# Modulation by pairs of tiles, split of the first weights, context's decays as columns, and a later place for the second modulation's first part

## The chip, the cores and the metric

The kernel runs on one core of a Trainium2 chip. The metric is the device time of one execution in microseconds; a comparison uses the median over several executions. TensorE (PE) multiplies, VectorE (DVE), ScalarE (ACT) and GpSimd (POOL) do elementwise work, and SyncE (SP) issues most of the transfers. Each engine works through its own row of instructions in order.

## The reference

One layer of a hybrid backbone with width D = 1024, 1024 latent tokens and 256 context tokens, 1280 in all. Cut to what matters:

```python
mod_x = silu(c) @ w_ada + b_ada            # six parts: sh1, sc1, g1, sh2, sc2, g2
mod_c = silu(c_ctx) @ w_ada + b_ada
px = modulate(rms_norm(x, norm1_w), sh1, sc1) @ w_in      # modulate: h * (1 + scale) + shift
pc = modulate(rms_norm(ctx, norm1_w), csh1, csc1) @ w_in
dn_c, s_f, s_b = gated_deltanet(pc[..., :DN_IN], ..., zero, zero)   # q, k, v, z, decays a, b
dn_x, _, _     = gated_deltanet(px[..., :DN_IN], ..., s_f, s_b)     # both directions, chunks of 64
na_x = neighborhood_attention(...)          # q, k with RMS norm, window keys and all context keys
x = x + g1 * (concat([dn_x, na_x]) @ w_out)
x = x + g2 * swiglu(modulate(rms_norm(x, norm2_w), sh2, sc2), w_ffn_in, w_ffn_out)
```

## The kernel before

Tokens lie along the free axis: x is eight tiles `xt0` to `xt7` of 128 features by 1280 tokens. A product in full precision is made of three in fp32r: each weight is split into `whi` (a cast, on ACT) and `wlo` (the rest, on POOL), each operand into `hh` and `hl`, and a block sums hh·whi, hl·whi and hh·wlo over the eight tiles (`mm_part`, L395).

*First stage.* SP loads c2, prm and the x tiles, then the first modulation's weights `wada` (eight tiles of 1 MB) and the raw weights `fraw` of the first two blocks; ACT's queue loads cw, qkw, onw, adt, cst and the masks. ACT squares each tile (L670), DVE adds the squares (L672), TensorE sums them over the partitions with ones (L675), ACT takes Ln and Exp of that. `ada(q)` makes a quarter of the first modulation: 16 products into one bank (L651), a copy `arow` on ACT (L654), a turn by four small products with `sel` (L657), an addition of the bias on DVE (L659). With the weights as they lie, ada(0) and ada(2) give scales, ada(1) and ada(3) shifts, each for four tiles. Then tile by tile: xt (L689) and hl (L692) on DVE, hh (L690) on ACT, and the products of the blocks `first` = k0, k1. SP's transfers take turns on a fixed set of semaphores, so an issue can wait for an earlier transfer of another queue.

*Jobs.* From then on a list of jobs is worked through: k2, k3, `Wide z 1`, (here `inv` = 5) nk0 to nk2, z0, nk3, nq0 to nq2, q0 to q3, nv0, v0, nv1, v1 to v3, nq3. A `Block` makes 128 features by all tokens. A `Wide` makes tokens by 256 or 264 columns (L578), with the tokens as stationary operand. The last 16 columns of z's second half are the decays `ab`; for the first two tiles of tokens, which are context, z itself is not needed, and the product is narrow (16 columns, L594). Beside the jobs run `Background` generators: `bg` (inverses of the blocks, decay tables, and from then on the preparations of the scans: `pr` products, kk L902, y L921), and `bg2`, the first four quarters of the second modulation. A quarter (`modulation`) loads eight tiles `wad` of 128 x 512, multiplies them by silu(c) and adds them up on DVE (L230, L232), and ends with four small products (L217) and an addition of the bias (modp, L219):

```python
        bg2.add(modulation(pools(bg2s, "adp", "left"), range(4), bank))
...
            if n == inv:
                bg2.drain()
```

The rest of the second modulation (quarters 4 to 7) follows in the last stages. Then come the scans and the attention (about 640 to 875 us), the output products with the gated output `oacc` (L1052, L1170; its pool `sp1`), and the feed-forward products, to the end. The scheduler that sets each engine's row may place an instruction earlier or later than it is written, as far as its operands allow.

Of the kernel before, what the change touches and what calls it, by code (L numbers as in the profile page):

```python
# [9 lines left out]
F32 = mybir.dt.float32  # L10
# [77 lines left out]
def hybrid(ctx, tc, a, dbg):  # L88
# [30 lines left out]
    sp.dma_start(c2, a["c2"])  # L119
    sp.dma_start(prm, a["prm"])  # L120
# [6 lines left out]
    act.dma_start(cw, a["cw"])  # L127
    qkw = const("qkw", [128, 2])
    act.dma_start(qkw, a["qkw"])
    onw = const("onw", [128, 1])  # L130
    act.dma_start(onw, a["onw"])
    adt = const("adt", [128, 16])
    act.dma_start(adt, a["adt"].rearrange("o d -> (o d)").partition_broadcast(128))
# [68 lines left out]
    def modulation(adp, qs, bank):  # L202
# [18 lines left out]
        for _ in range(3):  # L221
            fetch()
        prev = None
        for q in qs:
            acc2 = adp.tile([128, 512], F32, name="acc2", tag="acc2", bufs=2)
# [11 lines left out]
        for _ in range(6):  # L237
            yield
        reduce(qs[-1], prev)
# [127 lines left out]
    with ExitStack() as bs:  # L367
# [30 lines left out]
        class Block:  # L398
# [7 lines left out]
            def prefetch(self, raw=None):  # L406
# [3 lines left out]
                self.w = load_w(src, raw=raw)  # L410
# [143 lines left out]
        class Wide:  # L554
# [27 lines left out]
            def tiles(self):  # L582
# [26 lines left out]
        with ExitStack() as xs:  # L609
            xp = pools(xs, "xp", "left")  # L610
            xt = []
            act.dma_start(cst, a["cst"])
            masks = xp.tile([128, 4, 128], F32, name="masks", tag="masks")
            act.dma_start(masks, a["masks"])
# [12 lines left out]
            for j in range(4):  # L627
                load_ada(j)
            raws = [xp.tile([128, KT, 128], F32, name=f"fraw{i}", tag=f"fraw{i}") for i in range(2)]
            for i in range(2):  # L630
                sp.dma_start(raws[i], a["w_conv"][4 + i])
            for j in range(4, 8):
                load_ada(j)
            sel = xp.tile([128, 2], F32, name="sel", tag="sel")
            dve.tensor_reduce(sel, ident.rearrange("p (c i) -> p i c", i=32)[:, 0:2], AX.X, OP.add)
# [3 lines left out]
            act.copy(mr[:, 4], ident)  # L639
            for d in range(2):  # L640
                act.mul(mneg[:, d], masks[:, d], -1.0e30)
            act.copy(mr[:, 0:4], masks)
            rs = xp.tile([128, T], F32, name="rs", tag="rs")
            acc = xp.tile([128, T], F32, name="acc", tag="acc")
            def ada(q):
# [10 lines left out]
                for b in range(4):  # L656
                    pe.matmul(p[:, 2 * b:2 * b + 2], row[:, b * 128:(b + 1) * 128], sel, start=True, stop=True)  # L657
                b0 = 4 * (q // 2) + 8 * (1 - q % 2)
                dve.tensor_tensor(mod1[:, b0:b0 + 4], p[:, 0:8].rearrange("p (b c) -> p b c", c=2),  # L659
                                  bada[:, b0:b0 + 4].rearrange("p (b c) -> p b c", c=1).to_broadcast([128, 4, 2]),  # L660
                                  OP.add)
                if q % 2 == 0:
                    b = b0 - 8
                    dve.scalar_tensor_tensor(w1s[:, b:b + 4], mod1[:, b0:b0 + 4], 1.0,
                                             n1w[:, b:b + 4].rearrange("p (b c) -> p b c", c=1).to_broadcast(
                                                 [128, 4, 2]), op0=OP.add, op1=OP.mult)

            for k in range(KT):
                sq = xp.tile([128, T], F32, name="sq", tag="sq", bufs=2)
                act.activation(sq if k else acc, xt[k], AF.Square)  # L670
                if k:
                    dve.tensor_tensor(acc, acc, sq, OP.add)  # L672
            for s0, n in SEGS:
                p = bank()
                pe.matmul(p[:, :n], M[C_ONE], acc[:, s0:s0 + n], start=True, stop=True)  # L675
                act.activation(rs[:, s0:s0 + n], p[:, :n], AF.Ln, bias=b_eps, scale=1.0 / D)
            act.activation(rs, rs, AF.Exp, scale=-0.5)
            first[0].prefetch(raws[0])
            ada(0)
            ada(1)  # L680
            first[1].prefetch(raws[1])
            for k in range(KT):
# [13 lines left out]
                if k == 1:  # L696
# [976 lines left out]
```

## Time and profile before

| | before |
|---|---|
| runs | 1618.23, 1617.94, 1624.84 us, median 1618.23 |
| profiled execution | 1618.78 us, its span 1617.0 us |
| mean granted clock of TensorE | 0.979 |
| TensorE busy | 1512.7 us |
| DVE, ACT, POOL busy | 1039.2, 706.2, 210.8 us |
| first dense products of k0 (chain) | 45.66 us |

The page gives busy times, and 40 slices of the span, 40.4 us each. The chain follows the work that ended last back to its releasers; a row there holds start, duration and what ran. A row of the timeline holds start, duration, engine, line, operation and tiles, and in brackets the idle time before it and what ended it. A row of grouped lines ends with total, mean in ns, and idle time before. A row of windows holds the stretch, its length, the busy time of PE, the weight loads, DVE, ACT and POOL with their counts, then the granted clock, the share of DMA and GB/s.

### The profile page before, as it was taken

To read this page: it belongs to the slowest core of one execution; us is meant where nothing else is said; L and a number is where in the kernel's file an instruction comes from. 1 tells how busy PE (TensorE), PEld (TensorE's weight loads), DVE (VectorE), ACT (ScalarE), POOL (GpSimd) and SP (SyncE) were. 2 spreads that over 40 slices of the span, in tenths; PEclk is the share of its full clock that TensorE was granted. 3 is DMA by queue.
4 is the path that set the end of the run, shared out by engine and by line. 5 is a ranking of instruction groups with operands and counts; after the bars stand their busy time and mean duration, and the time that the engine had idled before them with its cause. 6 is when DMAs were issued, how large, how long until landed. Compare 5 with 4: busy or idle time off the path is not lost.

```text
span 1617.0 us, 24090 instructions
## 1 busy us (share of the span) xinstructions
PE 1512.7 (94%) x8642; PEld 1275.1 (79%) x8642; DVE 1039.2 (64%) x1931; ACT 706.2 (44%) x1341; POOL 210.8 (13%) x279
## 2 busy tenths in 40 slices
PE   2899899999989798999898999999999999999999
PEld 1689787778888786888787787888888888888887
DVE  4785678445264467577898638966656656679652
ACT  5353363663332234666674337433333333444441
POOL 0144611422232320111110000000000000000000
PEclk9898999999999899999999999999999999999999
DMA  9267121545346528999853910532223333698742
GB/s 370 89 209 218 56 76 40 177 129 173 120 126 194 185 95 212 312 282 283 234 178 119 324 46 33 196 105 98 98 98 110 101 109 113 231 365 307 253 157 85
DMA packets 206407, 271.03 MB, mean 168 GB/s; under 512 B 15952, under 2 KB 115792, under 8 KB 205264
## 3 DMA queue, kind: packets, MB, share of 16 engines
q1 hardware_dynamic: 200240, 264.14, 50.2%
q10 hardware_dynamic: 6048, 5.35, 1.0%
q8 instruction: 68, 1.11, 0.3%
q14 instruction: 51, 0.42, 0.1%
HBM read 204.68 MB, written 68.94 MB: 169 GB/s over the span
## 4 chain that ended last, share of the span: by engine, by line
PE 76%; DVE 10%; ACT 5%; DMA 4%; issue 2%; POOL 1%; SPq 0%; ACTq 0%; DVEq 0%; POOLq 0%
PE ps L1249 26%; PE ps L1592 13%; PE blk L395 11%; PE blk L578 4%; PE pr L920 3%; PE ps L1376 3%; PE sc L316 2%; PE sc L306 2%; PE sc L294 2%; DVE N L826 1%; DMA at<-qk_d 1%; DMA wad<-wa 1%; DVE tt L824 1%; DVE cacc L451 1%; PE pr L911 1%
## 5 line engine op out<-in xcount | busy, mean ns | idle before, releaser
L395 PE MATMUL blk<-hh,whi 128*128 128x512 f32 (+1 forms) x416 | 123.9, 390 | 1.4 <-ACT hh L690 1.0
L1310 ACT CAST uhi<-wq 128x512 fp32r<-128x512 f32 x101 | 60.4, 621 | 140.7 <-issue 61.6
L395 PE MATMUL blk<-hl,whi 128*128 128x512 f32 (+1 forms) x416 | 117.1, 374 | 5.0 <-DVE hl L692 5.0
L1310 ACT CAST uhi<-ws 128x512 fp32r<-128x512 f32 x91 | 54.7, 622 | 152.9 <-PE ps L1249 74.2
L395 PE MATMUL blk<-hh,wlo 128*128 128x512 f32 (+1 forms) x416 | 117.7, 375 | 0.6 <-POOL wlo L198 0.6
L1311 DVE TENSOR_TENSOR ulo<-wq,uhi 128x512 fp32r<-128x512 f32 x101 | 67.1, 686 | 69.0 <-ACT uhi L1310 38.9
L1249 PE MATMUL ps<-hT,uhi 128*128 128x512 f32 x336 | 104.0, 391 | 3.1 <-ACT hT L1424 3.1
L1249 PE MATMUL ps<-hT,ulo 128*128 128x512 f32 x336 | 103.9, 390 | 0.0
L1249 PE MATMUL ps<-lT,uhi 128*128 128x512 f32 x336 | 103.9, 391 | 0.0
L578 PE MATMUL blk<-zhi,hh 128*128 128x256 f32 (+2 forms) x304 | 90.1, 296 | 0.0
L1249 PE MATMUL ps<-hB,uhi 128*128 128x512 f32 x288 | 89.3, 391 | 0.0
L1249 PE MATMUL ps<-lB,uhi 128*128 128x512 f32 x288 | 89.2, 391 | 0.0
L395 PEld LDWEIGHTS blk<-hl,whi 128*128 128x128 f32 x416 | 73.7, 192 | 19.6 <-DVE hl L692 5.3
L1249 PE MATMUL ps<-hB,ulo 128*128 128x512 f32 x288 | 89.1, 390 | 0.0
L578 PE MATMUL blk<-zhi,hl 128*128 128x256 f32 (+2 forms) x304 | 88.4, 291 | 0.0
L578 PE MATMUL blk<-zlo,hh 128*128 128x256 f32 (+2 forms) x304 | 87.7, 289 | 0.0
L395 PEld LDWEIGHTS blk<-hh,wlo 128*128 128x128 f32 x416 | 73.3, 191 | 16.0 <-issue 1.6
L1311 DVE TENSOR_TENSOR ulo<-ws,uhi 128x512 fp32r<-128x512 f32 x91 | 60.7, 685 | 37.8 <-ACT uhi L1310 29.4
L395 PEld LDWEIGHTS blk<-hh,whi 128*128 128x128 f32 x416 | 71.3, 193 | 15.2 <-issue 3.6
L1249 PEld LDWEIGHTS ps<-hT,uhi 128*128 128x128 f32 x336 | 63.1, 189 | 16.5 <-ACT hT L1424 3.5
L1249 PEld LDWEIGHTS ps<-lT,uhi 128*128 128x128 f32 x336 | 63.4, 189 | 13.3
L1249 PEld LDWEIGHTS ps<-hT,ulo 128*128 128x128 f32 x336 | 63.3, 189 | 13.2
(341 smaller groups left out, 3719.5 us busy)
## 6 DMA issues: line engine op xcount, KB each, us to landing
wq<-w_fo SPq DMA_DIRECT2D x99, 256.0 KB
wq<-w_gu SPq DMA_DIRECT2D x88, 256.0 KB
wad<-wa SPq DMA_DIRECT2D x64, 256.0 KB
bt<-rpb SPq DMA_DIRECT2D x64, 192.0 KB
t_d<-g SPq DMA_DIRECT2D x22, 512.0 KB
fr<-t_d SPq DMA_DIRECT2D x44, 256.0 KB
f_d<-g SPq DMA_DIRECT2D x33, 256.0 KB
fr<-f_d SPq DMA_DIRECT2D x33, 256.0 KB
```

The lines of the kernel that those rows point to most:

```text
L294: pe.matmul(sc[:, u * 640 + n0:u * 640 + n1], q, ks[i], start=i == 0, stop=i == 1)
L306: pe.transpose(sc[:, u * 640 + j * 128:u * 640 + (j + 1) * 128], bt[:, j * 128:(j + 1) * 128], ident)
L316: pe.matmul(sc[u * ND:u * ND + ND, 1280:1408], vv, pt[:, j * 128:(j + 1) * 128], start=j == 0, stop=j == 4)
L395: pe.matmul(o, ww[:, k], xx[k][:, s], start=k == 0 and j == 0, stop=k == KT - 1 and j == 2)
L451: dve.scalar_tensor_tensor(acc[:, d0:d1], raw[:, d0 + o:d1 + o], cw[:, blk, tap:tap + 1], acc[:, d0:d1], op0=OP.mult, op1=OP.add)
L578: pe.matmul(p[:, :c1 - c0], x[k][:, s], ww[:, k, c0:c1], start=k == 0 and j == 0, stop=k == KT - 1 and j == 2)
L920: pe.matmul(p[:, hs[h]], f[:, h], src[:, h], start=True, stop=True)
L1249: pe.matmul(o, w[wi][:, k], x[xi][:, k], start=first and k == 0 and j == 0, stop=k == n - 1 and j == 2, skip_group_check=True)
L1310: act.copy(hi, self.raw[key])
L1311: dve.tensor_tensor(lo, self.raw[key], hi.bitcast(F32), OP.subtract)
L1376: pe.matmul(o, w[wi][:, k], parts[xi][k][:, s], start=k == 0 and j == 0, stop=k == KT - 1 and j == 2)
L1592: pe.matmul(o[b], w[wi][:, b], F[xn, p][xi], start=n in (0, 1, 5) and p == 0 and j == 0, stop=p == NFB // 2 - 1 and j == 2, skip_group_che ...
```

## The change

- *Transfers at the start.* c2 and prm go to ACT's queue. cst, cw, masks, qkw, onw and adt go to SP: cst behind the x tiles, the others behind the last wada.
- *First modulation.* wa1 is laid out anew: each `ada(q)` gives shift and scale of tiles 2q and 2q + 1. ada(0) stands ahead of the loop over tiles, ada(1) to ada(3) behind tiles 0, 1 and 2.
- *Norm.* The last square is not added on DVE; TensorE sums it (three more products). The copies `mr` and `mneg` move behind tile 5. `sel` is made after the additions.
- *First weights.* The low parts of k0 and k1 are made on DVE, not on POOL.
- *Context's decays.* 24 products of 16 x 256 (decays by tokens) take the place of 48 of 128 x 16; a copy and two transposes turn them.
- *Second modulation, first part.* It has three wad buffers and one sum instead of four and two, each quarter's small products come four steps behind it, its pool stays, it is stepped only in Blocks past `inv` + 4 (the first is nq0), and drained ahead of the last job.
- *Last stages.* `sp1` moves to another side of the memory, and a pad is dropped.

```diff
     c2 = const("c2", [128, KT, 2])
-    sp.dma_start(c2, a["c2"])
-    sp.dma_start(prm, a["prm"])
+    act.dma_start(c2, a["c2"])
+    act.dma_start(prm, a["prm"])
...
-    act.dma_start(cw, a["cw"])
...
-    def modulation(adp, qs, bank):
+    def modulation(adp, qs, bank, bufs=4, sums=2):
...
-                x = adp.tile([128, 512], F32, name="wad", tag="wad", bufs=4)
+                x = adp.tile([128, 512], F32, name="wad", tag="wad", bufs=bufs)
...
-        for _ in range(6):
-            yield
-        reduce(qs[-1], prev)
+            if sums == 1:
+                for _ in range(4):
+                    yield
+                reduce(q, prev)
+                prev = None
+        if prev is not None:
+            for _ in range(6):
+                yield
+            reduce(qs[-1], prev)
...
-                    for t in range(2):
-                        p = self.wide(t, 248, 264)
-                        act.copy(ab[:, t], p[:, :16])
+                    p = bank("blk")
+                    for k in range(KT):
+                        for j, (ww, x) in enumerate(((self.hi, hh), (self.hi, hl), (self.lo, hh))):
+                            pe.matmul(p[:16, :CT], ww[:, k, 248:264], x[k][:, :CT], start=k == 0 and j == 0,
+                                      stop=k == KT - 1 and j == 2)
+                    abT = cp.tile([16, CT], F32, name="abT", tag="abT")
+                    act.copy(abT, p[:16, :CT])
...
+                    if half == 1 and t == 3:
+                        q = bank()
+                        for i in range(2):
+                            pe.transpose(q[:, i * 16:i * 16 + 16], abT[:, i * 128:i * 128 + 128], ident[:16, :16])
+                        act.copy(ab[:, 0:2].rearrange("p c d -> p (c d)"), q[:, :32])
...
-            act.dma_start(cst, a["cst"])
...
+            sp.dma_start(cst, a["cst"])
+            raws = [xp.tile([128, KT, 128], F32, name=f"fraw{i}", tag=f"fraw{i}") for i in range(2)]
+            for j in range(2):
                 load_ada(j)
...
-                b0 = 4 * (q // 2) + 8 * (1 - q % 2)
...
+                k = slice(2 * q, 2 * q + 2)
+                m = mod1.rearrange("p (s b) c -> p s b c", s=2)[:, :, k]
...
-                if k:
+                if 0 < k < KT - 1:
                     dve.tensor_tensor(acc, acc, sq, OP.add)
...
+            for i, x in enumerate((acc, sq)):
+                for p, (s0, n) in zip(sums, SEGS):
+                    pe.matmul(p[:, :n], M[C_ONE], x[:, s0:s0 + n], start=i == 0, stop=i == 1)
...
-            first[0].prefetch(raws[0])
             ada(0)
-            ada(1)
-            first[1].prefetch(raws[1])
+            for b, raw in zip(first, raws):
+                b.prefetch(raw, dve)
...
-                if k == 1:
-                    ada(2)
-                    ada(3)
+                if k < 3:
+                    ada(k + 1)
...
-        bg2.add(modulation(pools(bg2s, "adp", "left"), range(4), bank))
+        bg2.add(modulation(adp, range(4), bank, 3, 1))
...
             if n == inv:
-                bg2.drain()
-                bg2s.close()
...
             if n == len(jobs) - 1:
                 bg.drain()
+                bg2.drain()
...
-                    bg2.step(2)
...
-                    bg2.step(1)
+                    if n > inv + 4:
+                        bg2.step(1)
...
-    sp1 = pools(stream, "sp1", "right")
...
-    shift(stream, "npad", "right", 96)
...
-    o["wa1"] = c(wada[:, :2048].reshape(8, 128, 4, 512).transpose(2, 1, 0, 3)[[2, 0, 3, 1]])
+    o["wa1"] = c(wada[:, :2048].reshape(8, 128, 2, 4, 256).transpose(3, 1, 0, 2, 4).reshape(4, 128, 8, 512))
```

The order on the engines, before and after (line, operation, tiles; the numbers behind names tell buffers apart). TensorE from its first instruction, before:

```order
L675 MATMUL m<-acc,ones 128x256
L675 MATMUL m<-acc,ones 128x512 x2
L651 MATMUL pm<-wada,wide 32x512 x8
L657 MATMUL pm<-sel,arow 128x2 x4
L651 MATMUL pm<-wada,wide 32x512 x8
L657 MATMUL pm<-sel,arow 128x2 x4
L395 MATMUL blk<-hh_132,whi 128x256
L395 MATMUL blk<-hl_133,whi 128x256
```

And after:

```order
L687 MATMUL m<-acc,ones 128x256
L687 MATMUL m<-acc,ones 128x512 x2
L687 MATMUL m<-sq,ones 128x256
L687 MATMUL m<-sq,ones 128x512 x2
L662 MATMUL pm<-wada,wide 32x512 x8
L668 MATMUL pm<-sel,arow 128x2 x4
L397 MATMUL blk<-hh_128,whi 128x256
L397 MATMUL blk<-hh_128,whi 128x512 x2
```

Three products of the sum came in, and one of the two groups of the modulation that stood ahead of the blocks moved in among them. VectorE behind the additions of the squares, before:

```order
L659 TENSOR_TENSOR mod_103<-pm,prm 128x8
L664 SCALAR_TENSOR_TENSOR w1s<-mod_103,prm 128x8
L689 SCALAR_TENSOR_TENSOR xt_149<-xt_149,w1s,rs 128x256
L689 SCALAR_TENSOR_TENSOR xt_149<-xt_149,w1s,rs 128x1024
L689 SCALAR_TENSOR_TENSOR xt_151<-xt_151,w1s,rs 128x256
L689 SCALAR_TENSOR_TENSOR xt_151<-xt_151,w1s,rs 128x1024
L689 SCALAR_TENSOR_TENSOR xt_153<-xt_153,w1s,rs 128x256
L689 SCALAR_TENSOR_TENSOR xt_153<-xt_153,w1s,rs 128x1024
L659 TENSOR_TENSOR mod_103<-pm,prm 128x8
L689 SCALAR_TENSOR_TENSOR xt_155<-xt_155,w1s,rs 128x256
L689 SCALAR_TENSOR_TENSOR xt_155<-xt_155,w1s,rs 128x1024
L692 SCALAR_TENSOR_TENSOR hl_133<-xt_149,mod_103,hh_132 128x256
```

And after:

```order
L682 TENSOR_TENSOR acc<-acc,sq 128x1280 x6
L683 TENSOR_REDUCE sel<-cst 128x2
L194 TENSOR_TENSOR wlo<-fraw_160,whi 128x1024
L671 TENSOR_TENSOR mod_99<-pm,prm 128x2x4
L674 SCALAR_TENSOR_TENSOR w1s<-mod_99,prm 128x4
L701 SCALAR_TENSOR_TENSOR xt_143<-xt_143,w1s,rs 128x256
L701 SCALAR_TENSOR_TENSOR xt_143<-xt_143,w1s,rs 128x1024
L194 TENSOR_TENSOR wlo<-fraw_161,whi 128x1024
L704 SCALAR_TENSOR_TENSOR hl_129<-xt_143,mod_99,hh_128 128x256
```

hl of the first tile stood behind xt of four tiles; now it stands behind its own xt and a split. VectorE at the end of job 4, where the decay tables begin (gA, L720; after, L737), before:

```order
L546 TENSOR_REDUCE SV<-kd 128x10
L230 TENSOR_SCALAR acc_1183<-wad,sc_104 128x512
L232 SCALAR_TENSOR_TENSOR acc_1183<-wad,sc_104,acc_1183 128x512 x7
L219 TENSOR_TENSOR modp<-m,prm 128x4 x2
L720 TENSOR_TENSOR gA<-ab,adt 128x40 x2
```

And after:

```order
L548 TENSOR_REDUCE SV<-kd 128x10
L439 SCALAR_TENSOR_TENSOR cacc<-blk,cw,cacc 128x512
L548 TENSOR_REDUCE SV<-kd 128x10
L737 TENSOR_TENSOR gA<-ab,adt 128x40 x2
```

Modulation's additions and their ends are gone from ahead of the tables. A part of them, after, on VectorE beside the first preparations (kk L919, y L938):

```order
L215 TENSOR_TENSOR modp<-m,prm 128x4
L226 TENSOR_SCALAR acc_2501<-wad,sc_100 128x512
L228 SCALAR_TENSOR_TENSOR acc_2501<-wad,sc_100,acc_2501 128x512 x2
L492 SCALAR_TENSOR_TENSOR cacc<-cacc,qkw,cr 128x1024
L919 SCALAR_TENSOR_TENSOR kk<-kk,NB,y 128x128 x4
L505 TENSOR_TENSOR hl_2559<-cacc,hl_2559 128x512 x2
L919 SCALAR_TENSOR_TENSOR kk<-kk,NB,y 128x128 x4
L938 TENSOR_TENSOR y<-pr,x_2148 128x512
L228 SCALAR_TENSOR_TENSOR acc_2501<-wad,sc_100,acc_2501 128x512 x2
```

The first quarter's eight additions (acc_2292) still stand in the jobs k2 to z1; those of the other three quarters, 24, stand here and behind. The loads of the same place, on SP's queue after:

```order
L207 DMA wad<-wa 128x512 x2
L510 DMA nq_d<-hl_2559 64x1024 x4
L207 DMA wad<-wa 128x512 x3
L192 DMA wraw<-w_conv 128x8x128
L207 DMA wad<-wa 128x512
L947 DMA y_d<-y 128x512
L207 DMA wad<-wa 128x512
L888 DMA kk<-kk_d 128x512
L207 DMA wad<-wa 128x512
L947 DMA y_d<-y 128x512
```

They stand between weights, stores of y and loads of kk, where before this queue had none of modulation's loads.

More of the change, by code (lines that the diff above doesn't have):

```diff
@@ L219, in reduce @@
             dve.tensor_tensor(modp[:, s], p[:, 0:4], bada[:, s], OP.add)
-        for _ in range(3):
+        for _ in range(bufs - 1):
             fetch()
@@ L224, in modulation @@
         for q in qs:
-            acc2 = adp.tile([128, 512], F32, name="acc2", tag="acc2", bufs=2)
+            acc2 = adp.tile([128, 512], F32, name="acc2", tag="acc2", bufs=sums)
             for k in range(KT):
@@ L404, in __init__, with prefetch @@
                 self.t0 = self.segs[0][0]
-            def prefetch(self, raw=None):
+            def prefetch(self, raw=None, lo_engine=pool):
                 i = self.i
@@ L638, in hybrid @@
             pool.tensor_copy(wide[:, :, 0:2], sc2)
[L639 to L642, printed above, removed]
+            sel = xp.tile([128, 2], F32, name="sel", tag="sel")
             rs = xp.tile([128, T], F32, name="rs", tag="rs")
```

46 lines of the change are left out of this document (24 added, 22 removed).

## The prediction

> **What bounds the kernel now.** I read the page first, for the engine that carries the span.
>
> ```profile
> span 1617.0 us, 24090 instructions
> PE 1512.7 (94%) x8642; PEld 1275.1 (79%) x8642; DVE 1039.2 (64%) x1931; ACT 706.2 (44%) x1341; POOL 210.8 (13%) x279
> PE   2899899999989798999898999999999999999999
> PEclk9898999999999899999999999999999999999999
> ```
>
> TensorE is busy 94% of the span, so a change pays where it takes work off TensorE or closes one of its gaps. The first slice of 40 us is busy only two tenths. The second and the fourth show a clock of 8 tenths. The chain of the first 60 us tells what fills the first slice.
>
> ```profile
> 2.63 8.31 DMA cst<-cst
> ...
> 14.41 1.27 ACT sq L670
> ...
> 25.24 3.94 PE m L675 x6
> ...
> 34.55 4.87 DVE xt L689 x6
> ...
> 39.49 5.71 DVE xt L689 x2
> ...
> 45.66 8.52 PE blk L395 x35
> 54.18 1.85 PE pm L651 x16
> ...
> 56.92 0.92 PE pm L657 x8
> ```
>
> The constants (cst) hold ACT's first work on data until 2.63 + 8.31 = 10.94. Squares and their sum then run until 25.24, the norm and the first modulation until 34.55, and VectorE forms xt and hl until dense products begin at 45.66. Who waits, for TensorE and for SyncE's queue (total, times, longest):
>
> ```profile
> PE m L675 <- DVE acc L672: 25.2, 1, 25.2
> ...
> PE pm L657 <- ACT arow L654: 2.7, 2, 2.0
> SPq L625 <- DMA cst<-cst: 2.8, 1, 2.8
> SPq L625 <- DMA onw<-onw: 1.9, 1, 1.9
> ```
>
> The last two rows are issues of the x tiles that stand behind small loads of ACT's queue.
>
> **First stage.** Rows by form within 0 to 81 us (total, mean ns); one split of a weight on VectorE from later on; one stretch of two microseconds (its last column GB/s); and, from the whole chain, the products that end the first two blocks:
>
> ```profile
> L672 DVE TENSOR_TENSOR acc<-acc,sq 128x1280 f32<-128x1280 f32 x7 | 10.4, 1493 | 3.6 <-ACT sq L670 3.1
> L689 DVE SCALAR_TENSOR_TENSOR xt<-xt,w1s,rs 128x1024 f32<-128x1024 f32 x8 | 12.3, 1538 | 0.0
> L692 DVE SCALAR_TENSOR_TENSOR hl<-xt,mod,hh 128x1024 fp32r<-128x1024 f32 x8 | 10.2, 1275 | 0.8 <-ACT hh L690 0.8
> L197 ACT CAST whi<-fraw 128x1024 fp32r<-128x1024 f32 x2 | 2.1, 1040 | 0.0
> ```
>
> ```profile
> 899.67 1.21 DVE L198 TENSOR_TENSOR wlo<-wraw,whi 128x1024 fp32r<-128x1024 f32 x1
> ```
>
> ```profile
> 8.00:10.00 2.00, 0.00 (x0) 0.00 (x0) 0.00 (x0) 0.00 (x0) 0.00 (x0) 1.00 1.02 416
> ```
>
> ```profile
> 62.43 16.77 PE blk L395 x85
> ```
>
> *Start of the norm's sum.* An x tile is 128 x 1280 x 4 bytes, 0.655 MB, so 1.58 us at 416 GB/s. With the eight issued first and none behind a small load, and data from about 3 us (an estimate: the first is issued in the second microsecond), the seventh lands at 14.0. Its square takes 1.27, its addition (the sixth) 1.49: 16.8, and the sum on TensorE starts at about 17.1 instead of 25.24. The eighth square, landed at 15.6, is ready by then. Gain so far 8.1.
>
> *From there to the first xt.* Before, 25.24 to 34.55, 9.3 us. After, three more matmuls of the sum stand in it (the eighth square goes to TensorE): no row has the second half of such a pair, so between nothing saved (3.94 again) and half of that; I take 2.9. whi of the first weight stands ahead of the Exp's table, 1.04. So 17.1 + 9.3 + 2.9 + 1.0 = 30.3 for the first xt, against 34.55.
>
> *Dense start.* Before, VectorE formed xt of four tiles before the first hl (4.87 and 5.71 us, the last tile's two parts drawn out while POOL split weights), and TensorE started at 45.66. After, tile 0 alone goes first: xt takes 1.6 (a third of the 4.87 for three tiles), hh on ACT follows part by part, and products with whi can go at about 32.9, an estimate of 1 us behind xt. The split of the second weight, 1.21 on VectorE now, lies between xt and hl of tile 0; that of the first runs beside the Exp on ACT.
>
> *End of the two blocks.* Before, 45.66 to 62.43 + 16.77 = 79.2, that is 33.5 us, with two of the four modulation groups inside; one group is 16 products of L651 (1.9) and a turn of 0.92, together 2.8. So the blocks alone are 33.5 - 5.6 = 27.9. After, three groups lie inside: 32.9 + 27.9 + 8.4 = 69.2 if TensorE never waits. It will: VectorE needs about 3.4 us a tile (xt 1.6, hl 1.28 and its part of 256 columns, some 0.4), TensorE 27.9 / 8 = 3.5, and the copy that feeds a turn (arow) now stands behind hh on ACT three times where 2.7 us of such waits stood before. I add 3.2: 72.4. **-6.8 us**, between -10 (no wait) and -4 (6 us of waits). Arrival of the modulation's weights is not what ends last: 5.24 MB of x, 0.33 of cst, 2.1 and 1.05 MB at 416 GB/s are in by 24, the group for tiles 2 and 3 by 29.
>
> **Second stage, 80 to 162 us.** The chain of the whole span, then TensorE's rows at the end of the stage, and three windows (busy PE, PEld, DVE, ACT, POOL, then clock, DMA share, GB/s):
>
> ```profile
> 117.11 6.87 PE blk L578 x48
> 126.44 5.00 PE blk L578 x24
> 131.88 2.94 PE blk L578 x24
> ```
>
> ```profile
> 124.73 1.71 PE L217 MATMUL m<-ones,acc 128*128 128x1 f32 x8
> 157.41 0.95 PE L217 MATMUL m<-ones,acc 128*128 128x1 f32 x8
> 160.66 1.02 PE L217 MATMUL m<-ones,acc 128*128 128x1 f32 x8 [0.85 <-DVE modp L219]
> 162.03 0.82 PE L395 MATMUL blk<-hh,whi 128*128 128x256 f32 x3 [0.35 <-DVE modp L219]
> ```
>
> ```profile
> 120.00:130.00 10.00, 10.00 (x51) 10.00 (x51) 9.93 (x15) 2.32 (x6) 8.73 (x11) 0.52 0.54 180
> 290.00:345.00 55.00, 50.53 (x260) 40.27 (x259) 25.88 (x37) 33.17 (x57) 27.09 (x45) 0.97 0.43 135
> 345.00:430.00 85.00, 84.69 (x543) 76.23 (x542) 34.25 (x41) 34.60 (x49) 14.65 (x6) 0.98 0.45 146
> ```
>
> TensorE has no gap here, so what is taken off it counts in full.
> - The 48 products of 16 columns (6.87) become 24 of 256 columns; 24 of 264 columns took 2.94. -3.9. Two small transposes and a copy come in, +0.3.
> - The clock fell to half behind the narrow products, though TensorE was busy throughout, and the next 24 products took 5.00 instead of 2.94. I expect that the spell goes with them: -2.1, and -0.4 for transposes that ran in it.
> - The four sums of modulation (L217) leave the stage: 1.6 and three of 0.8: -4.0. The waits behind them, 0.85 and 0.35, go: -1.2.
>
> Together **-11.3**, between -8 (the clock falls anyway) and -12.
>
> **Where modulation's first part goes.** Eight of its 32 additions stay early; 24 additions with their loads, and the four sums, now stand between 290 and 430 us. VectorE's row for one addition, what VectorE waited for its loads before, and two pairs of rows of the stage where they land:
>
> ```profile
> L232 DVE SCALAR_TENSOR_TENSOR acc<-wad,sc,acc x28: 750/752/3326, 73.5 to 159.8; 128x512 f32<-128x512 f32 x28
> DVE acc L232 <- DMA wad<-wa: 19.3, 8, 11.3
> 305.61 2.75 DVE L902 SCALAR_TENSOR_TENSOR kk<-kk,NB,y 128x128 f32<-128x128 f32 x4 [0.68 <-ACT y L900]
> 315.95 1.27 DVE L902 SCALAR_TENSOR_TENSOR kk<-kk,NB,y 128x128 f32<-128x128 f32 x4 [2.50 <-ACT y L900]
> ```
>
> The sums cost TensorE 4 x 0.8 again: +3.2. The additions are 24 x 0.75 = 18 us on VectorE, which is busy 60 of these 140 us. Their cover is that slack; if it is gone, products wait for kk (L902) or y (L921) behind an addition, 0.75 at a time. On SyncE's queue 24 loads now stand between stores of y, loads of kk and xc for the preparations, and the weights of the next blocks; with three buffers, each waits until an earlier addition is done, and so do those behind it. Bounds: 0 and +8 (below); I take **+2**, nearer the low end since TensorE has a gap of only 4.5 us in the first window and 0.3 in the second. The loads leave 80 to 162 us, where TensorE waited for none but the last (counted).
>
> POOL now and then doubles an operation of VectorE here: the first L902 row ran beside POOL, the second not. That is a price for the eight additions that stand in the first window, where POOL is busy half the time: 8 x 0.75 more is 6; the other sixteen meet it 17% of the time: 2. All on the path, +8. The Trainium skill, "SBUF — State Buffer", section "Who interferes with whom", has it that an operation of VectorE with two inputs in SBUF and one of GpSimd that reads SBUF exclude each other for the whole of an instruction; by that rule every addition is a candidate, and the sum would come out 6 higher. The L902 rows agree with it.
>
> **Two small ones.** After the scans, eight additions (second modulation's) no longer stand in VectorE's last chain before oacc, and TensorE's wait there goes; and the decay tables need no longer stand behind modulation's last additions, which can shorten the two waits below them.
>
> ```profile
> 889.37 1.12 PE L1052 MATMUL ps<-cst,oacc 128*128 128x128 f32 x4 [2.03 <-DVE oacc L1170]
> PE m L836 <- DVE N L830: 3.6, 1, 3.6
> PE m L795 <- POOL rc L782: 2.7, 3, 1.8
> ```
>
> **-2** (0 to -2) for the first; **-1** for the second (0 to -6.3, both waits gone), since the tables move only about 2 us against the products beside them.
>
> Sum: -6.8 - 11.3 + 3.2 + 2 - 2 - 1 = -15.9. The profiled execution took 1618.78 (its span is 1617.0), so 1602.9; the median shown is 1618.23, 0.55 lower, so 1602.3 beside it. I say 1602.
>
> **The rivals.**
> - *More comes.* No waits in the first stage (-10) and both waits of the decays' chain gone (-6.3): 1602 - 3.2 - 5.3 = 1593.5. For it: both queues of work shrink where the waits are. Against: the second wait's chain (L826 to L830) is VectorE's own and as long as before.
> - *Contention.* The additions meet POOL as above, +8 instead of +2: 1608. For it the L902 rows; against it that most of VectorE's work here waits for something else anyway.
> - *The start doesn't move as far.* ACT carries squares, whi, three Ln, hh and arow in one line; if each group's arow adds 3 us of wait on TensorE (three times, beside the 3.2), the first stage gains nothing: 1602 + 6.8 = 1609. For it the 2.7 of arow waits; against it that VectorE is relieved of 10.6 us before the first product.
> - *Slower.* The loads of modulation's first part hold up SyncE's queue in 290 to 430 us: before, VectorE waited 19.3 us for eight of them, 2.4 each. The 24 come in groups of three buffers, eight groups. If each group delays kk, xc or a weight by more than 3 us, the 15.9 and 8.1 more are gone (8 x 3.0 = 24): slower than 1626. With the longest of those waits, 11.3, at four groups it is 1602 + 45 - 2 = 1645. Against it: TensorE's two windows have other work in order (whole blocks of products), and DMA is 45% busy.
>
> **How the numbers follow.** Chances: forecast 0.53; more 0.12; contention 0.17; start 0.10; the loads' queue 0.08, half of it past 1626. No change that can be told is 0.5%, 8.1 us: 1610.1 to 1626.3. Contention and start lie at 1608 and 1609 with a third of each above 1610 (0.09), half of the queue's case lies between (0.04). So faster 0.83, same 0.13, slower 0.04. The range holds the forecast, most of the more-case and the two middle ones: 1593 to 1611. The forecast's own range is 1597 to 1606: first stage from -10 to -4, second from -12 to -8.
>
> **What the profile after would show.** The sum of the norm starts near 17 and dense products near 33; the first two blocks end near 72. Between 110 and 130 no products of 16 columns, and a clock near 1.00. Behind z's last products the next block without sums of modulation between them. Rows of wad additions between 290 and 430 with TensorE's gaps there as before (4.5 and 0.3 us); no wait of 2 us at oacc. Wrong if: TensorE's gaps in 290 to 430 grow by more than 8, the clock falls between 100 and 125 again, or the dense start stays above 38.

## The result, and the profile after

| | before | after |
|---|---|---|
| median | 1619.05 us (6 runs, 1617.94 to 1627.83) | 1604.86 us (6 runs, 1601.58 to 1610.41) |
| ratio | | 0.990, 95% interval 0.9875 to 0.9925 |
| profiled execution, span | 1618.78, 1617.0 | 1603.61, 1601.8 |
| mean granted clock | 0.979 | 0.983 |

The kernel became 14 us faster, by the medians. The page of the changed kernel, its first parts:

```profile
span 1601.8 us, 24051 instructions
...
PE 1509.9 (94%) x8626; PEld 1269.3 (79%) x8626; DVE 1038.7 (65%) x1934; ACT 706.1 (44%) x1341; POOL 205.5 (13%) x277
...
PE   4999999899898897999899999999999999999999
...
PEclk8999999999999999999999999999999999999999
```

TensorE's busy time fell by 2.8 us only; the rest of the 15.2 us of span was idle time, 10.2 of it ahead of the first product of k2 (idle 33.9 us of 81.4 before, 23.7 of 75.4 after); the first slice is busy four tenths instead of two. The clock's dip in the fourth slice is gone; the first slice now shows 8 tenths. TensorE's timeline in the first stage:

```profile
17.94 4.64 PE L687 MATMUL m<-acc,ones 128*128 128x256 f32 x6 [17.94 <-DVE acc L682]
22.37 2.57 PE L687 MATMUL m<-sq,ones 128*128 128x256 f32 x6
24.87 1.92 PE L662 MATMUL pm<-wada,wide 128*32 128x512 f32 x16
29.70 1.87 PE L668 MATMUL pm<-sel,arow 128*128 128x2 f32 x8 [2.91 <-ACT arow L665]
33.16 0.58 PE L397 MATMUL blk<-hh,whi 128*128 128x256 f32 x1 [1.59 <-ACT hh L702]
```

From 30 to 76 us TensorE has these waits alone, the first of them for the first turn:

```profile
PE pm L668 <- ACT arow L665: 2.9, 1, 2.9
PE blk L397 <- ACT hh L702: 2.8, 2, 1.6
```

The sum starts 7.3 us earlier, the first dense product 6.9 (33.16 for 40.09) and the second 10.7 (34.99 for 45.66). Windows of four microseconds at the start, two of ten around the decays, and the two of the later stage, moved by the 15 us that lie ahead of them (busy PE, PEld, DVE, ACT, POOL, then clock, DMA share, GB/s):

```profile
28.00:32.00 4.00, 1.87 (x8) 1.78 (x8) 0.33 (x2) 2.59 (x3) 0.00 (x0) 0.71 1.00 418
32.00:36.00 4.00, 1.59 (x3) 1.12 (x4) 3.92 (x5) 1.66 (x2) 0.00 (x0) 0.50 1.02 424
36.00:40.00 4.00, 4.00 (x11) 1.91 (x9) 3.18 (x5) 1.66 (x2) 0.00 (x0) 0.51 1.04 377
```

```profile
110.00:120.00 10.00, 10.00 (x87) 9.40 (x86) 3.93 (x8) 6.37 (x13) 4.82 (x2) 1.00 0.74 224
120.00:130.00 10.00, 10.00 (x85) 9.84 (x85) 4.55 (x6) 3.34 (x10) 3.65 (x9) 1.00 0.62 203
```

```profile
275.00:330.00 55.00, 50.37 (x266) 39.41 (x265) 37.03 (x51) 31.81 (x56) 28.05 (x45) 0.97 0.57 177
330.00:415.00 85.00, 84.18 (x544) 75.78 (x543) 44.07 (x56) 32.51 (x46) 12.90 (x5) 0.98 0.56 178
```

The first blocks run at half clock until 40. Around the decays (110.8 to 114) and behind them the clock is whole; before, the ten microseconds from 120 held 51 products at 0.52, now they hold 85. In the later stage VectorE's busy time grew by 21 us (60.1 to 81.1) while TensorE's gaps stayed: 4.6 and 0.8 us, against 4.5 and 0.3. And the ends of three stages on TensorE, before and after:

```profile
81.37 0.51 PE L395 MATMUL blk<-hh,whi 128*128 128x256 f32 x2
```

```profile
75.38 0.51 PE L397 MATMUL blk<-hh,whi 128*128 128x256 f32 x2
...
110.78 0.36 PE L598 MATMUL blk<-hh,zhi 128*16 128x256 f32 x1
...
113.96 0.37 PE L580 MATMUL blk<-zhi,hh 128*128 128x264 f32 x1
...
141.81 2.39 PE L541 MATMUL m<-cacc 128*128 128x128 f32 x20
145.59 0.85 PE L397 MATMUL blk<-hh,whi 128*128 128x256 f32 x3 [1.39 <-ACT kk L542]
...
874.66 1.03 PE L1068 MATMUL ps<-cst,oacc 128*128 128x128 f32 x8
```

The first row of each is the first product of k2. The decays take 3.2 us up to the first wide product instead of 9.4 (116.9 to 126.3, with a sum of modulation of 1.7 in it), and nk0 starts at 145.59 instead of 162.03. oacc's turn runs in one piece; the 2.03 us of wait are gone.

### The profile page after: what moved, and what is told of

The parts are those of the page before. It is cut to its first block, busy times and chain, and to the rows that moved or that the text cites. A ratio compares the mean times of both kernels' runs of the same rounds, so it can differ in the third digit from the quotient of the medians.

```text
span 1601.8 us, 24051 instructions
## 1 busy us (share of the span) xinstructions
PE 1509.9 (94%) x8626; PEld 1269.3 (79%) x8626; DVE 1038.7 (65%) x1934; ACT 706.1 (44%) x1341; POOL 205.5 (13%) x277
## 5 line engine op out<-in xcount | busy, mean ns | idle before, releaser
L397 PEld LDWEIGHTS blk<-hl,whi 128*128 128x128 f32 x416 | 73.5, 192 | 15.2 <-issue 1.7
L397 PEld LDWEIGHTS blk<-hh,wlo 128*128 128x128 f32 x416 | 73.3, 191 | 15.2 <-POOL wlo L194 0.9
L580 PE MATMUL blk<-zhi,hh 128*128 128x256 f32 (+1 forms) x288 | 84.4, 293 | 0.0
L580 PE MATMUL blk<-zhi,hl 128*128 128x256 f32 (+1 forms) x288 | 82.9, 288 | 0.0
L580 PE MATMUL blk<-zlo,hh 128*128 128x256 f32 (+1 forms) x288 | 82.2, 285 | 0.0
L193 ACT CAST whi<-wraw 128x1024 fp32r<-128x1024 f32 x26 | 27.3, 1048 | 112.7 <-PE blk L397 55.7
```

Of the source, the lines that this page charges most:

```text
L193: act.copy(h, r)
L397: pe.matmul(o, ww[:, k], xx[k][:, s], start=k == 0 and j == 0, stop=k == KT - 1 and j == 2)
L580: pe.matmul(p[:, :c1 - c0], x[k][:, s], ww[:, k, c0:c1], start=k == 0 and j == 0, stop=k == KT - 1 and j == 2)
```

## The experiments

For each run these starts on TensorE come from the timeline of its profiled execution: z1 is the first product of the decays, nk0 the first of job 5, pr the first of the preparations, z0 the last product of the Wide jobs, oacc the first and last turn of oacc, end the last product.

| kernel | z1 | nk0 | pr | z0 | oacc | end |
|---|---|---|---|---|---|---|
| before | 116.9 | 162.0 | 302.5 | 536.4 | 789.9, 890.2 | 1612.8 |
| after | 110.8 | 145.6 | 287.3 | 524.5 | 778.1, 875.4 | 1597.6 |
| decays alone | 116.8 | 158.3 | 300.9 | 536.4 | 790.2, 890.6 | 1615.6 |
| modulation later alone | 116.1 | 156.2 | 298.4 | 537.4 | 792.6, 892.6 | 1615.2 |
| first stage alone | 111.1 | 156.7 | 298.3 | 532.3 | 788.8, 888.5 | 1611.1 |
| oacc's pool alone | 115.0 | 160.3 | 300.9 | 532.9 | 788.6, 886.1 | 1608.2 |
| after, modulation as before | 109.4 | 155.8 | 298.1 | 532.4 | 785.8, 883.3 | 1605.5 |
| after, idle products | 109.0 | 143.9 | 285.7 | 526.6 | 782.1, 879.7 | 1601.9 |
| after, last square on VectorE | 108.3 | 143.2 | 285.9 | 521.8 | 779.8, 878.5 | 1600.6 |
| after, split on GpSimd | 109.7 | 146.7 | 288.5 | 524.1 | 779.7, 877.2 | 1599.4 |
| after, last square and first arow on VectorE | 107.5 | 143.0 | 285.8 | 522.2 | 780.4, 877.7 | 1600.2 |
| after, these two and idle products | 108.6 | 143.2 | 285.1 | 523.5 | 779.3, 876.7 | 1598.8 |
| after, few additions | 110.6 | 145.7 | 287.6 | 525.2 | 781.2, 878.5 | 1600.6 |
| before, 64 columns | 116.6 | 160.7 | 302.3 | 536.8 | 793.0, 893.1 | 1615.7 |

Each row is one execution. Four of these kernels (before, decays alone, oacc's pool alone, 64 columns) have the same code up to z1 and reach it between 115.0 and 116.9: a difference of 1.9 us at z1 is scatter between executions. From pr to the first oacc, kernels with the same code in that stretch differ by up to 5.6. Four kernels (last square, split, last square with first arow, 64 columns) were run once, at 1606.60, 1605.35, 1606.17 and 1621.94 us; of them only the stages are compared.

**The parts, each alone on the kernel before.** The edits are the pieces of the diff above: the decays (L589 to L601), the second modulation's first part (`modulation`, its pool, its steps and its drain), the first stage (transfers, `ada`, the last square, the split), and sp1 with npad.

> The kernel before with the context's decays as columns alone. Theory A (the narrow products let the clock fall, and the columns do away with that): the 48 products of 6.87 us become about 2.9, and the next 24 take 2.9 instead of 5.0, so with the transposes in that spell the span shrinks by 6 to 7 us, and the clock is 1.00 from 110 to 130. Theory B (the clock falls there anyway, for another reason, such as the sums of modulation that follow): 3.5 to 4 us, and a window of 0.5 stays.

Measured 0.9965 (0.9945 to 0.9986), median 1616.21 against 1621.57. The clock is whole, as theory A has it, and z1 to its last product is 32.6 us instead of 39.5, 7.0 less:

```profile
120.00:130.00 10.00, 10.00 (x85) 9.83 (x84) 9.89 (x17) 4.41 (x11) 8.47 (x10) 1.00 0.64 199
```

But of these 7.0 only 3.7 arrive at nk0. TensorE reaches the drain of modulation earlier now and waits there 4.2 us, where it waited 0.85; the drain's additions wait for their loads:

```profile
PE m L217 <- DVE modp L219: 4.2, 1, 4.2
...
DVE acc L232 <- DMA wad<-wa: 12.4, 6, 3.3
```

> The kernel before with the later place of the second modulation's first part alone (three buffers, one sum). Theory A (it is a move of work that TensorE has to do anyway, and what is gained is the waits behind it): 80 to 162 us gain about 5 us (four sums and 1.2 of waits), 290 to 430 lose 3 to 4; in all -1 to -2 us, and the half clock at 120 to 130 stays. Theory B (the additions and loads cost the later stage as much as they spared): 0, with longer waits of the preparations' products.

Measured 1.001 (0.9985 to 1.0036): nothing, as theory B has it for the whole. In the profile both halves are there: nk0 5.8 us earlier, and z0 1.0 later. The half clock came without modulation's sums between, so these were not its cause; it ended sooner, so that the second row took 3.98, where it took 5.00 before and takes 2.94 at the full clock (chain of waits):

```profile
116.38 6.92 PE blk L584 x48
...
124.27 3.98 PE blk L584 x24
```

> The first stage's changes alone (order of transfers, modulation by pairs, last square on TensorE, split of the first weights on VectorE), all else as before. Theory A (TensorE runs at half clock until about 40 us since it waited just ahead): the two blocks end 4 us earlier, as in the changed kernel, and the whole gains 4 us. Theory B (the stage is longer in the changed kernel only by what else was changed): 6 to 7 us, as forecast.

Measured 0.9984 (0.996 to 1.0008). z1 is 5.8 us earlier, as in the changed kernel (6.1), nearer theory B; the 4 us of theory A came from a misread end of the blocks (see below); the median shows 1 to 3 us of it, within its uncertainty, and nk0 in the profile 5.4. What becomes of it behind pr can't be told from one profile.

> The move of oacc's pool alone, all else as before. Theory A (its old place bound the order of the second modulation's additions to VectorE's last chain): the additions stand behind the chain, the wait of 2.0 us for oacc goes, and 2 to 3 us are gained. Theory B (the additions of quarters 4 and 5 are needed soon after, and a wait for them takes its place): 0.

Measured 0.998 (0.9957 to 1.0003), which doesn't tell 2 us from none. The profile has theory A: from the first to the last oacc it is 97.4 us instead of 100.2, 2.8 less, and 97.3 to 97.6 in the other kernels with the moved pool (98.7 in one), and the additions stand behind VectorE's last chain (its end and their first; before, they began at 879.90 and the chain ended at 890.1):

```profile
882.60 1.14 DVE L1170 SCALAR_TENSOR_TENSOR oacc<-oacc,orr,z 128x128 f32<-128x128 f32 x4
...
887.97 0.48 DVE L230 TENSOR_SCALAR acc<-wad,sc 128x512 f32<-128x512 f32 x1
```

The last turn on TensorE runs in one piece:

```profile
885.29 1.03 PE L1052 MATMUL ps<-cst,oacc 128*128 128x128 f32 x8
```

The four ratios multiply to 0.994, the whole is 0.990. The intervals, 0.002 to 0.003 to each side, don't show this difference by themselves; that two of the parts work together, and where, the next run shows.

**The changed kernel with modulation's first part as before.**

```diff
-        bg2.add(modulation(adp, range(4), bank, 3, 1))
+        bg2.add(modulation(pools(bg2s, "adp", "left"), range(4), bank))
...
             if n == inv:
+                bg2.drain()
```

> The changed kernel with the second modulation's first part where and as it was before (four buffers, two sums, drained ahead of job 5). Theory A (with the decays' 4 us of narrow products gone, the drain's loads end later than the products that covered them, as the columns alone showed: 8.9 us from the last z product to the next block instead of 5.6): the wait ahead of nk0 is 8 us or more against 3.9, and 3 to 5 us of the gain at nk0 are lost; of these 3 come back until the last z product at 524, so the whole is 0 to 2 us slower than the changed kernel. Theory B (the later place costs what it spares in any company): nk0 is later by 5 and the whole level.

Measured 0.9928 (0.9907 to 0.9948), median 1612.62 us, where the changed kernel has 0.990 and 1604.86. By the ratios it is 4.5 us slower, but their intervals overlap; by the ends of the profiled executions 7.8 (1605.5 against 1597.6). The clearest comparison is with the kernel with idle products below, which is level with the changed kernel and was measured beside this one: 1606.89 (1603.56 to 1609.89) against 1612.62 (1611.51 to 1614.25), 5.7 us, and no two runs cross. I had expected 0 to 2. From the last z product to nk0 it is 13.7 us instead of 3.9 (before: 5.6). Timeline of TensorE and waits of VectorE:

```profile
153.59 1.84 PE L213 MATMUL m<-ones,acc 128*128 128x1 f32 x8 [8.11 <-DVE modp L215]
155.77 1.40 PE L391 MATMUL blk<-hh,whi 128*128 128x256 f32 x3 [0.34 <-DVE modp L215]
```

```profile
DVE acc L228 <- DMA wad<-wa: 11.0, 7, 3.0
```

The shorter first stage and the quicker decays had taken away the cover of these loads: the last z product starts 14.3 us earlier than before (142.07 against 156.40), the last of the 32 additions only 9.5 (150.3 against 159.8). The loads are not all of the wait. The last three additions met an operation of GpSimd that before had started as they ended (160.39); timelines of VectorE and of GpSimd:

```profile
148.62 4.82 DVE L228 SCALAR_TENSOR_TENSOR acc<-wad,sc,acc 128x512 f32<-128x512 f32 x3 [1.89 <-DMA wad<-wa]
```

```profile
149.95 2.94 POOL L540 TENSOR_TENSOR kd<-kk,cst 128x1280 f32<-128x1280 f32 x1 [8.72 <-ACT nA L726]
```

Three additions take 2.25 us elsewhere, so some 2.6 of the 8.1 are this meeting. Behind the wait the clock was at half from 152 to 160, which costs more behind nk0. So the move is worth nothing that can be told alone (1.001) and 5 to 8 us in company.

**Which products let the clock fall.** The two context tiles' products with 64 columns, of which the same 16 are used:

```diff
-                        p = self.wide(t, 248, 264)
-                        act.copy(ab[:, t], p[:, :16])
+                        p = self.wide(t, 200, 264)
+                        act.copy(ab[:, t], p[:, 48:64])
```

> The kernel before with the two context tiles' decays made by products of 64 columns instead of 16, as many of them; of the result the same 16 columns are used. Theory A (the clock fell because the array has little to do in products of 16 columns): with four times the columns it stays at 1.00 from 110 to 130, and the next 24 products take 2.9 us instead of 5.0, though the 48 take no less time each. Theory B (it fell for another reason at that place, or products below 128 columns all do it): a spell of half clock stands there as before.

Theory B: products of 64 columns do it too. That it is the place instead is spoken against by the decays as columns alone, with which the clock stayed whole there. The chain of waits:

```profile
116.87 6.88 PE blk L578 x48
...
126.17 5.03 PE blk L578 x24
```

Four times the columns took the same time, 6.88, and the clock fell just so. So 64 columns aren't enough to hold the clock when each product takes a weight of its own; with 264 columns and a weight each, z's products held it (85 in ten microseconds, above). Where between them it turns wasn't tried.

**The later place: is its price the additions?** This kernel leaves out 21 of the 24 late additions and their loads, so its result is not the reference's:

```diff
-        order = [(q, k) for q in qs for k in range(KT)]
+        KS = lambda q: 1 if q in (1, 2, 3) else KT
+        order = [(q, k) for q in qs for k in range(KS(q))]
...
-            for k in range(KT):
+            for k in range(KS(q)):
```

> The changed kernel with 21 of the 24 late additions and their loads left out (the second to fourth quarter use one of their eight weight tiles, so gate and shift values are not the reference's); the four sums on TensorE stay. From the first product of the preparations to z's last product the changed kernel takes 237.2 us and the kernel before 233.9; over all kernels so far 235.6 to 240.9 with the late place and 232.1 to 235.5 with the early one. Theory A (most of the 3.6 between them is the sums, 3 x 0.8): the stretch stays at 236 to 237, the whole within 2 us of 1605. Theory B (additions, loads and their places in the queues cost as much as the sums or more): the stretch falls to 233 to 235, the whole to 1600 to 1602.

Measured 1604.36 us, 0.9884 (0.9863 to 0.9905), against 1604.86 and 0.990: theory A in the median; by the ratios it is 2.6 us faster, within the intervals. The stretch from pr to z0 in three windows, of before, of after and of this kernel (third column of times: VectorE's busy time):

```profile
302.48:536.42 233.94, 216.64 (x1391) 193.92 (x1392) 115.29 (x170) 92.67 (x174) 77.25 (x105) 0.95 0.47 148
```

```profile
287.28:524.46 237.18, 218.28 (x1416) 194.65 (x1417) 132.42 (x194) 92.59 (x174) 79.01 (x105) 0.96 0.54 167
```

```profile
287.65:525.23 237.58, 217.42 (x1409) 195.16 (x1410) 116.37 (x171) 92.67 (x174) 77.34 (x105) 0.96 0.46 144
```

16 us less on VectorE and 5.5 MB less of transfers change nothing that can be told (237.6 against 237.2, in a stretch that scatters by 5 among like kernels). A price of 2 or 3 us isn't excluded by this; one of 8 would stand out, since the stretch is 3.2 us longer than before with the sums in it. The additions did meet GpSimd. In the changed kernel those of L228 in the later place (their count, then the shortest, median and longest in ns):

```profile
L228 DVE SCALAR_TENSOR_TENSOR acc<-wad,sc,acc x21: 737/751/2908, 280.8 to 361.8; 128x512 f32<-128x512 f32 x21
```

The 21 took 21.8 us, where 21 of 0.75 are 15.8: four of them took 1.5 to 2.9 beside an operation of GpSimd. These 6 us are most of the 8 that the contention rival counted; that they fell into VectorE's slack is what the stretch shows, within its scatter.

**The first stage.** Idle products in TensorE's waits:

```diff
+            def spin(n):
+                d = bank()
+                for _ in range(n):
+                    pe.matmul(d[:, :256], M[C_ONE], acc[:, 0:256], start=True, stop=True)
...
                 act.copy(row, p)
+                if q == 0:
+                    spin(6)
...
             ada(0)
+            spin(4)
```

> The changed kernel with ten idle products more on TensorE (six in its wait for the first arow, four behind the first turn), whose results nothing uses. Theory A (the clock is at half from 29 to 40 us because TensorE stood idle from 26.8 to 33, and the first blocks pay for that): the clock stays near 1.00 there, z1 starts 2 to 4 us earlier than in the changed kernel, which is the difference between the 4.1 us that the first stage gained and the 6.8 forecast. Theory B (the first stage is bound by VectorE's and ACT's line of xt, hh and hl): z1 starts where it did, within 1 us, or later, since the idle products push the blocks back.

The clock was held:

```profile
28.00:32.00 4.00, 3.87 (x22) 3.21 (x21) 1.12 (x3) 2.65 (x3) 0.00 (x0) 1.00 1.01 420
32.00:36.00 4.00, 2.35 (x10) 1.43 (x10) 4.00 (x7) 2.09 (x4) 0.00 (x0) 1.00 1.01 422
```

z1 came at 109.0, against 109.4 to 110.8 in the kernels without: 0.4 to 1.8 us, within the scatter. Between 32 and 36 TensorE is busy 2.35 of 4 us while VectorE is busy throughout: at the full clock the blocks wait for hh and hl (1.65 us). So theory B holds, as far as the scatter lets it be told. (The 4.1 us that theory A started from is the misread end of the blocks again: the first stage gained 6.0.) The whole: 1606.89, 0.9889 (0.9867 to 0.991), level with the changed kernel.

The last square on VectorE (`if k:` for `if 0 < k < KT - 1:`, and TensorE sums `acc` alone):

> The changed kernel with the last square added on VectorE again, so that TensorE has three products of the sum instead of six. Theory A (the three more products cost what they take, 2.5 us, and the spared addition is 1.5): the modulation's first product starts about 1 us earlier than the 24.87 of the changed kernel. Theory B (the longer sum keeps the clock up and the addition stands on the path): it starts later or level, and the half clock begins sooner.

```profile
22.77 1.92 PE L662 MATMUL pm<-wada,wide 128*32 128x512 f32 x16
```

Theory A: 22.77 against 24.87. With the same code ahead the start scatters, from 23.6 to 24.9 in six kernels with the square on TensorE and from 22.8 to 23.7 in the three with it on VectorE; by the means it is 1.2 us. z1 came at 108.3 (107.5 to 108.6 in the three, 109.0 to 111.1 in the six). This part of the change cost 1 to 2 us where it stands; that the whole would gain it isn't shown.

The split on GpSimd again (`b.prefetch(raw, pool)`):

> The changed kernel with the low parts of the first two weights made on GpSimd again. Theory A (VectorE and GpSimd block each other: VectorE's xt of 1024 columns took up to 2.5 us beside GpSimd's splits before, 1.28 in the changed kernel): xt and hl of the first tiles take 2 us and more, the first dense products start level or earlier, but z1 starts 1 to 3 us later. Theory B (GpSimd was free, and VectorE is relieved of 2.4 us): z1 starts 1 to 2 us earlier.

z1 at 109.7 is within the scatter: neither theory can be told. GpSimd's splits ran ahead of xt, and only one small operation of VectorE met the second: w1s, which took 0.16 in the changed kernel. Timelines of GpSimd and of VectorE:

```profile
29.41 2.34 POOL L194 TENSOR_TENSOR wlo<-fraw,whi 128x1024 fp32r<-128x1024 f32 x1 [1.65 <-ACT whi L193]
```

```profile
30.55 1.22 DVE L674 SCALAR_TENSOR_TENSOR w1s<-mod,prm 128x4 f32<-128x4 f32 x1
```

Before, GpSimd's splits came later (38.19 to 44.1) and met xt, two of which took 5.79 together. By the Trainium skill ("SBUF — State Buffer", section "Who interferes with whom") an operation of VectorE with two inputs in SBUF, as w1s is, is held until an instruction of GpSimd that reads SBUF and came first is done. The rows agree: the split ended at 31.75, w1s at 31.77.

The last square and the first arow, both on VectorE (`dve.tensor_copy(row, p)` where q is 0):

> The changed kernel with the last square added on VectorE and the first arow copied by VectorE, which stands idle then, instead of ACT. Theory A (xt of the first tile waits for the turn, 2.5 us behind the norm's Exp, since arow stood behind the Exp on ACT): the turn starts near 25.3 instead of 27.6 in the kernel with the square alone moved, xt 0.5 to 2.5 us earlier, z1 as much earlier than 108.3. Theory B (what ends last ahead of xt is then the split of the weights, behind whi on ACT): the turn comes earlier but z1 stays within 0.7 of 108.3.

```profile
25.02 0.69 DVE L666 COPY arow<-pm 128x512 f32<-128x512 f32 x1 [6.02 <-PE pm L662]
...
28.58 1.22 DVE L194 TENSOR_TENSOR wlo<-fraw,whi 128x1024 fp32r<-128x1024 f32 x1
29.72 1.67 DVE L704 SCALAR_TENSOR_TENSOR xt<-xt,w1s,rs 128x256 f32<-128x256 f32 x2
```

Theory B, nearly: the copy ends at 25.7, but xt starts at 29.72, 0.4 earlier than in the run before (30.13), since the splits stand ahead of it behind whi; z1 at 107.5, 0.75 earlier, less than the scatter. And with idle products besides:

> All three together: last square added on VectorE, first arow copied by VectorE, and eight idle products on TensorE (two ahead of the first turn, six behind it). Theory A (each gains in its own place): z1 starts at 105 to 107, against 110.8 in the changed kernel, and the whole is 3 to 6 us faster than it, near 1600. Theory B (what is gained at z1 is given back in the later stages, where loads and VectorE's chains end last): z1 earlier, but the whole within 2 us of 1605.

Measured 1604.80, 0.9893 (0.9867 to 0.9919). Theory B: z1 at 108.6 and nk0 at 143.2, 2.2 to 2.4 us earlier than after, and the whole level. No version beat the changed kernel by what its measurement can tell.

## Why the prediction was right, and where its terms were off

Predicted 1602, measured 1604.86, within the forecast's own range. By the terms, in the profiled executions (in us):

| term | forecast | measured | from |
|---|---|---|---|
| first stage, to the first product of k2 | -6.8 | -6.0 | 81.37 to 75.38 |
| second stage, to nk0 | -11.3 | -10.5 | 80.7 to 70.2 us long |
| later place, nk0 to the first oacc (decays' chain in it) | +3.2 +2 -1 | +4.6 | 627.9 to 632.5 |
| oacc | -2 | -2.9 | 100.2 to 97.3 |
| from there to the end | 0 | -0.4 | 722.6 to 722.2 |
| sum | -15.9 | -15.2 | |

- *Start of the sum:* 17.1 forecast, 17.94 measured. Sum and its three more products: 6.84 forecast, 6.93 measured. That the last square would be some 1 us better on VectorE was not seen.
- *First xt:* 30.3 forecast, 32.08 measured. I let the turn follow Exp at once; arow stood behind whi and Exp on ACT, and the turn of eight small products then took 1.87 instead of 1.05 at a falling clock.
- *End of the blocks:* two errors that met. 79.2 was the point at which ACT was released, not the last product, which ended at 81.4; so "72.4" stands for 74.6 and the measured 75.38 is 0.8 later. The 3.2 us for TensorE's waits were near the right size, but not for their reason: no turn behind the first dense product waited for its arow. TensorE waited 1.25 us for hh at 34.99 and not at all from 36 to 74 (busy 38.00 of 38.00). From 33.16 to 75.38 it is 42.2 us; blocks and groups, with the right end, are 35.7 - 5.6 + 8.4 = 38.5, so 3.7 more. What the wait doesn't account for lies with the half clock up to 40, which the forecast left out; with the clock held, waits for hh and hl took its place, and z1 gained less than 2 us. That the size fitted is luck.
- *Decays:* columns and clock came as forecast; z1 took 8.6 us less, sums included. The spell was the narrow products' own (it came without the sums too, and with 64 columns).
- *Waits behind the sums:* the forecast let 1.2 us go and put nothing in their place. A wait of 1.39 for kk (L542) took it; before, the drain stood in that place.
- *Later place:* the forecast's +2 for the additions was not borne out: leaving 21 of them out changed the time by nothing that can be told, though 2 us are less than these runs can tell. The -1 for the decays' chain came: its two waits went from 3.6 and 2.7 us to 3.6 and 1.8. The 1.4 us beyond the four sums lie within the scatter of that stretch; what they are stays open. The rival of contention fell in its price, not in its mechanism: the additions were 6 us longer beside GpSimd, and TensorE didn't wait for them. Of its two L902 rows the second, read as clear of GpSimd, overlapped it too, for 0.3 us (315.95 to 316.29). The rival of SyncE's queue fell as well: with 21 loads fewer the stretch was as long.
- *What the forecast didn't have:* the sum treats the terms as independent. Without the move, the whole is 5 to 8 us slower, since the other parts then run into the drain. That the sum came out is in part luck: the change held the one part that the others needed. The profile of before could have hinted at it: VectorE waited 19.3 us for these loads, and the cover of these waits was the time that the other parts took away.

## What to carry to other kernels

A stage that waits for loads in its shadow has a price that shows only when the shadow gets shorter: move such loads in the same step as the speed-up, and price each part against the others, not against the kernel before. Here 24 additions on an engine with slack cost nothing that could be told, even where GpSimd drew them out; at a drain that TensorE waits for, three additions that met GpSimd lengthened the wait by 2.6 us. What counts is the work and the waits that they put on the bound engine. Ahead of the first dense stage, follow one engine's line of small operations (here ACT: Ln, a cast, a table, Exp, a copy): a step that is moved off one engine helps by what the next in the line leaves.

## What the runs showed of the hardware

Products of 16 and of 64 columns, each with a weight of its own, took the same 6.9 us for 48, and about 3.6 us after the first (116.86) TensorE's clock fell to half, though the profile has it busy all the time. The timeline of the kernel before, at that point; start to start it goes from 0.11 to 0.21:

```profile
120.33 0.26 PE L578 MATMUL blk<-zhi,hl 128*128 128x16 f32 x1
120.44 0.34 PE L578 MATMUL blk<-zlo,hh 128*128 128x16 f32 x1
120.63 0.36 PE L578 MATMUL blk<-zhi,hh 128*128 128x16 f32 x1
120.84 0.36 PE L578 MATMUL blk<-zhi,hl 128*128 128x16 f32 x1
```

With products of 256 columns on 16 weights' columns (24 in 2.8 us) it stayed whole; but 2.8 us is less than those 3.6, so this doesn't show that such products would hold it for longer. The Trainium skill, "TensorE: Matmul & The Clock Gate", section "Part 1: The HAM clock gate (the "warmup" mystery)", has the gate follow how busy TensorE has been; here the profile's busy time was 10.00 of 10.00 us at a clock of 0.52 and didn't tell. That products with few columns count for little is a reading of these runs, not shown by them.
